# A rotary embedding kernel: six slabs in flight, and casts, products and sum inside the slab's own bytes

## The chip, the cores and the metric

The kernel runs on one core of a Trainium2 chip. The time is the device time of one execution in microseconds (us). Three runs of the kernel before took 162.06, 162.46 and 162.85 us; the median is 162.46.

The engines are called as in the profile: PE (TensorE), DVE (VectorE), ACT (ScalarE), POOL (GpSimd) and SP (SyncE). A letter q behind an engine's name stands for its sequencer, which waits and issues DMAs.

## What is computed

The input x has 16 batches of 512 positions with 16 heads of 64 values. In each head the two halves are rotated by the position's angles:

```python
x = x.reshape(batch, seq, num_heads, head_dim)
x1, x2 = x[..., :half_dim], x[..., half_dim:]
cos = cos[None, :, None, :]
sin = sin[None, :, None, :]
rotated = np.concatenate([x1 * cos - x2 * sin,
                          x1 * sin + x2 * cos], axis=-1)
```

Input and output are float32, 33.55 MB each. cos and sin have 512 x 32 values each.

## The kernel before

The work is cut into eight slabs of two batches. A slab is a tile of 128 partitions by 8192 float32 values (32 KB per partition, 4.194 MB in all); each partition holds eight consecutive positions of 1024 values, so that a slab is one contiguous stretch of DRAM. A slab is loaded by one DMA (line 64), worked on, and stored by one DMA from the same tile (line 141).

The pool of slabs has five places (`slots`). Loads 0 to 4 are issued at the start by SP, with the two small tables behind load 0. Load s + 5 is asked for after store s, into the same place, and so waits until store s has landed. Loads 0 to 5 are issued by SP and loads 6 and 7 by POOL (line 62). Stores are issued by ACT, in ACT's own instruction stream.

Lines 81 to 103 make the table `tab`: cos and sin, for all 128 partitions, as bf16, the sine with a minus sign in the half where it is needed. That is done once, by POOL, PE and DVE.

A slab is worked on in passes (lines 118 to 121): slabs 0, 6 and 7 in two passes of four positions (4096 values per partition), called 0a, 0b, 6a, 6b, 7a and 7b in this document, and slabs 1 to 5 in one of eight (8192 values). A pass has five instructions:

- a cast by ACT from the float32 slab to a bf16 buffer `xb` (line 112, "cast 5" is that of slab 5);
- two products by DVE (line 133): `xb` times the sine goes to the first half of the pass's bytes in the slab (`t2`, seen as bf16), and `xb` times the cosine goes to `xb` itself;
- a sum by DVE (line 136) of `xb` and `t2` with its halves swapped, into `xb`;
- a widening by ACT from `xb` to the float32 slab (line 139, "copy 5").

There are two buffers `xb` of a whole slab (16 KB per partition each), so that the cast of slab s waits for the widening of slab s - 2.

The text asks for the cast of the next pass before the products of this one; each engine runs its instructions in a fixed list. The framework that builds the program makes these lists and the waits; on ACT it has put cast 1 ahead of both copies of slab 0, where the text has it between them, and it keeps to the text from there on.

The five and the two buffers take 5 x 32 + 2 x 16 = 192 KB per partition.

Of the kernel before, what the change touches and what calls it, by code (L numbers as in the profile page):

```python
# [2 lines left out]

# [4 lines left out]


@with_exitstack  # L10
def kernel(
    ctx: ExitStack,
    tc: tile.TileContext,
    x: bass.AP,
    cos: bass.AP,
    sin: bass.AP,
    num_heads: int,
    out: bass.AP,
):
    nc = tc.nc  # L20
    P = nc.NUM_PARTITIONS

    batch, seq, dim = x.shape
    nh = num_heads
    hd = dim // nh
    half = hd // 2
    bf16 = mybir.dt.bfloat16
    f32 = mybir.dt.float32

    nb = 2  # L30
    slots = 5
    nslabs = batch // nb
    rpp = nb * seq // P
    W = rpp * dim
    SP = seq // rpp
    TW = rpp * half

    out_flat = out.rearrange("b s h d -> b s (h d)")

    singles = ctx.enter_context(tc.tile_pool(name="singles", bufs=1))  # L40
    slabs = ctx.enter_context(tc.tile_pool(name="slabs", bufs=slots))
    xpool = ctx.enter_context(tc.tile_pool(name="xpool", bufs=2))
    psum = ctx.enter_context(tc.tile_pool(
        name="psum", bufs=1, space=bass.MemoryType.PSUM))


    def dram(t, s, a=0, n=W):
        return bass.AP(tensor=t.tensor, offset=t.offset + s * nb * seq * dim + a,
                       ap=[[W, P], [1, n]])


    def view(t, offset, *dims):
        return dataclasses.replace(t, offset=t.offset + offset,
                                   ap=[t.ap[0], *[list(d) for d in dims]])


    slab = {}


    def load(s):  # L60

        queue = nc.sync if s < nslabs - 2 else nc.gpsimd
        slab[s] = slabs.tile([P, W], f32, tag="slab", name="slab")
        queue.dma_start(out=slab[s], in_=dram(x, s))  # L64


    load(0)


    cos_sb = singles.tile([SP, TW], f32, tag="cos_sb")  # L70
    sin_sb = singles.tile([SP, TW], f32, tag="sin_sb")
    for t, src in ((cos_sb, cos), (sin_sb, sin)):
        nc.sync.dma_start(out=t, in_=bass.AP(  # L73
            tensor=src.tensor, offset=src.offset, ap=[[TW, SP], [1, TW]]))

    for s in range(1, slots):
        load(s)

    pick = singles.tile([SP, 2 * P], bf16, tag="pick")
    nc.gpsimd.memset(pick, 0.0)  # L82
    for g in range(2):
        part = view(pick, g * P, (SP, P // SP), (1, SP))
        nc.gpsimd.affine_select(  # L85
            out=part, in_=part, compare_op=mybir.AluOpType.not_equal,
            fill=1.0 - 2.0 * g, base=0, pattern=[[0, P // SP], [-1, SP]],
            channel_multiplier=1)

    tab1 = singles.tile([SP, 2 * TW], bf16, tag="tab1")  # L90
    for i, t in enumerate((cos_sb, sin_sb)):
        nc.gpsimd.tensor_copy(out=view(tab1, i * TW, (1, TW)), in_=t)  # L92

    acc = psum.tile([P, 2 * rpp * hd], f32, tag="acc")
    for i in range(2):
        for h in range(2):
            nc.tensor.matmul(  # L97
                view(acc, i * rpp * hd + h * half, (hd, rpp), (1, half)),
                view(pick, i * h * P, (1, P)),
                view(tab1, i * TW, (half, rpp), (1, half)),  # L100
                start=True, stop=True)
    tab = singles.tile([P, 2 * rpp * hd], bf16, tag="tab")
    nc.vector.tensor_copy(out=tab, in_=acc)  # L103

    xb = {}


    def cast(u):
        s, r, n = u
        if r == 0:  # L110
            xb[s] = xpool.tile([P, W], bf16, tag="xb", name="xb")
        nc.scalar.copy(out=view(xb[s], r * dim, (1, n * dim)),  # L112
                       in_=view(slab[s], r * dim, (1, n * dim)))

    passes = []
    for s in range(nslabs):
        n = rpp if 1 <= s < nslabs - 2 else rpp // 2  # L120
        passes += [(s, r, n) for r in range(0, rpp, n)]


    cast(passes[0])
    for i, (s, r, n) in enumerate(passes):
        if i + 1 < len(passes):
            cast(passes[i + 1])
        xs = view(slab[s], r * dim, (1, n * dim))
        xu = view(xb[s], r * dim, (1, n * dim))

        t2 = view(slab[s].bitcast(bf16), 2 * r * dim, (1, n * dim))
        for t, a in ((t2, rpp * hd), (xu, 0)):
            nc.vector.tensor_mul(  # L133
                out=t, in0=xu,
                in1=view(tab, a + r * hd, (hd, n), (0, nh), (1, hd)))
        nc.vector.tensor_add(  # L136
            out=xu, in0=xu, in1=view(t2, half, (hd, n * nh), (-half, 2), (1, half)))

        nc.scalar.copy(out=xs, in_=xu)  # L139
        if r + n == rpp:  # L140
            nc.scalar.dma_start(out=dram(out_flat, s), in_=slab[s])  # L141
            if s + slots < nslabs:
                load(s + slots)


# [1 line left out]
_INS = ['x', 'cos', 'sin', 'num_heads']  # L147
_OUTS = [((16, 512, 16, 64), 'float32')]

_NUMBERS = {'num_heads': 16}  # L150


# [26 lines left out]
```

## Time and profile before

| what | value |
|---|---|
| median of three runs | 162.46 us |
| span of the profiled execution | 160.2 us |
| around the span (median less span) | 2.3 us |
| ACT busy | 113.5 us, 71% of the span, 23 instructions |
| DVE busy | 108.6 us, 68%, 34 instructions |
| POOL busy, PE busy | 3.0 us, 1.0 us |
| moved by DMA | 67.24 MB, mean 420 GB/s |
| DMA time of SP's, ACT's and POOL's queues, share of 16 engines | 37.5%, 48.5%, 12.1% |
| cast or widening on ACT, 128 x 8192 | 7.02 us |
| one product or sum on DVE, 128 x 8192 | 4.43 us |

The profile is of one execution; its own time beside the span isn't recorded, so the median stands for it. Times in it count from the first instruction. "Busy" is the time in which an engine runs an instruction. The line "DMA" of the page gives the mean busy share of the 16 DMA engines in each of 40 slices, in tenths, where 9 is 90% or more. In the timeline a line has the start, the duration, the engine, the line of the kernel, the operation, the tiles and shapes, and in brackets the idle time before it with what ended it. A line for several instructions shows the time from the first start to the last end. "To landing" is the time from a DMA's issue to its last byte's arrival.

### The profile page before, as it was taken

The numbers are of one execution on the slowest core, as the hardware profiler recorded it, in microseconds if no ns is written. First come the engines' busy times: TensorE is split into PE (matmuls) and PEld (weight loads), VectorE is DVE, ScalarE is ACT, GpSimd is POOL, SyncE is SP. The second block draws the span as 40 slices with busy tenths as digits, with TensorE's granted clock in tenths as the row PEclk, the third lists the DMA queues.
The fourth block names the chain that finished last, engine by engine and source line by source line (L and its number), as shares of the span: only waits on it lengthen the run. The fifth ranks groups of instructions, "written<-read, shape, count | busy, mean of one in ns | idle before, by whom it ended". The sixth has DMA issues, their size and how long they took to land.

```text
span 160.2 us, 159 instructions
## 1 busy us (share of the span) xinstructions
PE 1.0 (1%) x4; PEld 0.5 (0%) x4; DVE 108.6 (68%) x34; ACT 113.5 (71%) x23; POOL 3.0 (2%) x11
## 2 busy tenths in 40 slices
PE   0002000000000000000000000000000000000000
PEld 0000000000000000000000000000000000000000
DVE  0001899999979979997997299919839499940000
ACT  3006929998999999899919995089995999553000
POOL 2001000000000000000010001000000000000000
DMA  7999999999999999999999999999999999999995
GB/s 246 409 393 426 393 450 466 393 417 491 401 393 426 491 393 409 499 401 393 483 434 393 450 466 393 426 483 401 409 491 409 393 475 442 393 442 475 393 426 229
DMA packets 2464, 67.24 MB, mean 420 GB/s; under 512 B 288, under 2 KB 416, under 8 KB 416
## 3 DMA queue, kind: packets, MB, share of 16 engines
q10 hardware_dynamic: 1152, 33.55, 48.5%
q1 hardware_dynamic: 1024, 25.30, 37.5%
q0 software_dynamic: 288, 8.39, 12.1%
HBM read 33.69 MB, written 33.55 MB: 420 GB/s over the span
## 4 chain that ended last, share of the span: by engine, by line
DMA 49%; ACT 28%; issue 8%; DVE 4%; SPq 1%; ACTq 0%; POOLq 0%
DMA slab<-in_x_dram 29%; DMA out_dram<-slab 20%; ACT slab L139 16%; ACT xb L112 12%; DVE xb L136 1%; DVE xb L133 1%; DVE slab L133 1%; SPq L73 1%; ACTq L141 0%; SPq L64 0%; POOLq L174 0%; ACTq L139 0%; POOLq L64 0%
## 5 line engine op out<-in xcount | busy, mean ns | idle before, releaser
L112 ACT CAST xb<-slab 128x4096 bf16<-128x4096 f32 (+1 forms) x11 | 56.6, 5155 | 27.8 <-DMA slab<-in_x_dram 26.5
L139 ACT CAST slab<-xb 128x4096 f32<-128x4096 bf16 (+1 forms) x11 | 56.6, 5154 | 3.5 <-DVE xb L136 3.5
L133 DVE TENSOR_TENSOR slab<-xb,tab 128x4096 bf16<-128x4096 bf16 (+1 forms) x11 | 35.9, 3260 | 17.3 <-ACT xb L112 17.2
L133 DVE TENSOR_TENSOR xb<-xb,tab 128x4096 bf16<-128x4096 bf16 (+1 forms) x11 | 35.9, 3261 | 0.3
L136 DVE TENSOR_TENSOR xb<-xb,slab 128x4096 bf16<-128x4096 bf16 (+1 forms) x11 | 35.9, 3261 | 0.3
L103 DVE CAST tab<-acc 128x1024 bf16<-128x1024 f32 x1 | 1.2, 1225 | 15.2 <-PE acc L97 15.2
L64 POOL DMA_DIRECT2D slab<-in_x_dram x2 | 1.2, 608 | 84.1 <-DMA out_dram<-slab 84.1
L112 ACT ACT_TABLE_LOAD x1 | 1.3, 1283 | 0.7 <-PEq L160 0.7
L97 PE MATMUL acc<-tab,pick 64*128 64x256 bf16 x4 | 1.0, 402 | 14.2 <-POOL tab L92 14.2
L92 POOL CAST tab<-cos_sb 64x256 bf16<-64x256 f32 x1 | 0.4, 389 | 12.1 <-DMA cos_sb<-in_cos_dram 12.1
L85 POOL TENSOR_SCALAR_AFFINE_SELECT pick<-pick 64x128 bf16<-64x128 bf16 x2 | 0.5, 285 | 0.1
L97 PEld LDWEIGHTS <-pick 64*128 64x128 bf16 x4 | 0.5, 122 | 14.2 <-issue 12.6
L92 POOL CAST tab<-sin_sb 64x256 bf16<-64x256 f32 x1 | 0.4, 394 | 0.0
L82 POOL MEMSET pick<- 64x256 bf16 x1 | 0.3, 304 | 0.3 <-POOLq L160 0.3
L160 POOL MEMSET const-float32-0.0<- 128x1 f32 x1 | 0.1, 103 | 0.2 <-issue 0.2
L160 POOL MEMSET const-bfloat16-1.0<- 128x1 bf16 x1 | 0.1, 107 | 0.0
L160 POOL MEMSET const-uint8-127<- 128x1 uint8 x1 | 0.1, 106 | 0.0
L160 POOL MEMSET const-float32-1.0<- 128x1 f32 x1 | 0.1, 103 | 0.0
## 6 DMA issues: line engine op xcount, KB each, us to landing
out_dram<-slab ACTq DMA_DIRECT2D x8, 4096.0 KB, 25.9
slab<-in_x_dram SPq DMA_DIRECT2D x6, 4096.0 KB, 26.6
slab<-in_x_dram POOLq DMA_DIRECT2D x2, 4096.0 KB, 24.9
cos_sb<-in_cos_dram SPq DMA_DIRECT2D x1, 64.0 KB, 12.5
sin_sb<-in_sin_dram SPq DMA_DIRECT2D x1, 64.0 KB, 12.3
```

Of the source, the lines that this page charges most:

```text
L64: queue.dma_start(out=slab[s], in_=dram(x, s))
L73: nc.sync.dma_start(out=t, in_=bass.AP(tensor=src.tensor, offset=src.offset, ap=[[TW, SP], [1, TW]]))
L82: nc.gpsimd.memset(pick, 0.0)
L85: nc.gpsimd.affine_select(out=part, in_=part, compare_op=mybir.AluOpType.not_equal, fill=1.0 - 2.0 * g, base=0, pattern=[[0, P // SP], [-1 ...
L92: nc.gpsimd.tensor_copy(out=view(tab1, i * TW, (1, TW)), in_=t)
L97: nc.tensor.matmul(view(acc, i * rpp * hd + h * half, (hd, rpp), (1, half)), view(pick, i * h * P, (1, P)), view(tab1, i * TW, (half, rpp) ...
L103: nc.vector.tensor_copy(out=tab, in_=acc)
L112: nc.scalar.copy(out=view(xb[s], r * dim, (1, n * dim)), in_=view(slab[s], r * dim, (1, n * dim)))
L133: nc.vector.tensor_mul(out=t, in0=xu, in1=view(tab, a + r * hd, (hd, n), (0, nh), (1, hd)))
L136: nc.vector.tensor_add(out=xu, in0=xu, in1=view(t2, half, (hd, n * nh), (-half, 2), (1, half)))
L139: nc.scalar.copy(out=xs, in_=xu)
L160: nc = _bacc.Bacc("TRN2", target_bir_lowering=False, num_devices=1)
```

## The change

The pool of slabs gets a sixth place, and loads 0 to 5 are issued at the start. Load 6 follows store 0 and load 7 follows store 1. The condition that picks the queue now reads `s < slots`, which is s < 6 as before.

The two bf16 buffers are removed. The float32 bytes of a pass in the slab are now seen as two halves of bf16 values, `lo` and `up`, each as long as the pass. The cast reads the float32 values and writes them as bf16 to `lo`, the first half of the same bytes. The first product, with the cosine, goes from `lo` to `up`; the second, with the sine, goes from `lo` to `lo`. The sum adds `up` and `lo` with its halves swapped, into `up`. The widening reads `up` and writes the float32 values over the whole of the pass's bytes. Buffers take 6 x 32 = 192 KB per partition.

```diff
-    slots = 5
+    slots = 6
...
-    xpool = ctx.enter_context(tc.tile_pool(name="xpool", bufs=2))
...
-        queue = nc.sync if s < nslabs - 2 else nc.gpsimd
+        queue = nc.sync if s < slots else nc.gpsimd
...
-    xb = {}
-    def cast(u):
-        s, r, n = u
-        if r == 0:
-            xb[s] = xpool.tile([P, W], bf16, tag="xb", name="xb")
-        nc.scalar.copy(out=view(xb[s], r * dim, (1, n * dim)),
-                       in_=view(slab[s], r * dim, (1, n * dim)))
...
+    def halves(u):
+        s, r, n = u
+        t = slab[s].bitcast(bf16)
+        return [view(t, (2 * r + i * n) * dim, (1, n * dim)) for i in range(2)]
+    def cast(u):
+        s, r, n = u
+        nc.scalar.copy(out=halves(u)[0], in_=view(slab[s], r * dim, (1, n * dim)))
...
-        xs = view(slab[s], r * dim, (1, n * dim))
-        xu = view(xb[s], r * dim, (1, n * dim))
-
-        t2 = view(slab[s].bitcast(bf16), 2 * r * dim, (1, n * dim))
-        for t, a in ((t2, rpp * hd), (xu, 0)):
+        lo, up = halves(u)
+        for t, a in ((up, 0), (lo, rpp * hd)):
             nc.vector.tensor_mul(
-                out=t, in0=xu,
+                out=t, in0=lo,
                 in1=view(tab, a + r * hd, (hd, n), (0, nh), (1, hd)))
         nc.vector.tensor_add(
-            out=xu, in0=xu, in1=view(t2, half, (hd, n * nh), (-half, 2), (1, half)))
+            out=up, in0=up, in1=view(lo, half, (hd, n * nh), (-half, 2), (1, half)))
-        nc.scalar.copy(out=xs, in_=xu)
+        nc.scalar.copy(out=view(slab[s], r * dim, (1, n * dim)), in_=up)
```

More of the change, by code (lines that the diff above doesn't have):

```diff
@@ L121 @@
         passes += [(s, r, n) for r in range(0, rpp, n)]
+    def halves(u):
[5 more added lines that the diff above has]
+        nc.scalar.copy(out=halves(u)[0], in_=view(slab[s], r * dim, (1, n * dim)))
     cast(passes[0])
-    for i, (s, r, n) in enumerate(passes):
+    for i, u in enumerate(passes):
+        s, r, n = u
         if i + 1 < len(passes):
             cast(passes[i + 1])
-        xs = view(slab[s], r * dim, (1, n * dim))
-        xu = view(xb[s], r * dim, (1, n * dim))
-        t2 = view(slab[s].bitcast(bf16), 2 * r * dim, (1, n * dim))
-        for t, a in ((t2, rpp * hd), (xu, 0)):
+        lo, up = halves(u)
+        for t, a in ((up, 0), (lo, rpp * hd)):
             nc.vector.tensor_mul(
-                out=t, in0=xu,
+                out=t, in0=lo,
                 in1=view(tab, a + r * hd, (hd, n), (0, nh), (1, hd)))
         nc.vector.tensor_add(
-            out=xu, in0=xu, in1=view(t2, half, (hd, n * nh), (-half, 2), (1, half)))
-        nc.scalar.copy(out=xs, in_=xu)
+            out=up, in0=up, in1=view(lo, half, (hd, n * nh), (-half, 2), (1, half)))
+        nc.scalar.copy(out=view(slab[s], r * dim, (1, n * dim)), in_=up)
         if r + n == rpp:
```

## The prediction

> **What bounds the kernel now.** I read the page's DMA lines first, then the rate in one long stretch, then the timeline for the places where ScalarE (ACT) waits. The page, slices of 4 us:
>
> ```profile
> DVE  0001899999979979997997299919839499940000
> ACT  3006929998999999899919995089995999553000
> ...
> DMA  7999999999999999999999999999999999999995
> GB/s 246 409 393 426 393 450 466 393 417 491 401 393 426 491 393 409 499 401 393 483 434 393 450 466 393 426 483 401 409 491 409 393 475 442 393 442 475 393 426 229
> ...
> HBM read 33.69 MB, written 33.55 MB: 420 GB/s over the span
> ```
>
> The DMA line is full from the second slice to the last but one, while VectorE (DVE) and ACT have holes. The stretches view gives the rate in the middle, in its last column:
>
> ```profile
> 20.00:152.00 132.00, 0.00 (x0) 0.00 (x0) 104.41 (x32) 105.65 (x21) 1.22 (x2) 1.00 1.00 433
> ```
>
> So one slab of 4.194 MB takes 4.194/0.433 = 9.7 us when it has the DMA engines to itself. Sixteen slab transfers (8 in, 8 out) are 155 us; the other 5 us of the 160.2 us span are the start and the last landing. The same bytes move after the change. Hence the floor: **nothing that only moves transfers about can win more than the fraction of a microsecond that the DMA line lacks in the middle; what can happen is that the DMA engines run dry.** Where are they closest to that? At the end, when the last store is issued. I need the two landing summaries (first the loads' line, then the stores' line) and the timeline from there back:
>
> ```profile
> DMA to landing us min/median/max: 12.6/24.9/60.8
> ```
>
> ```profile
> DMA to landing us min/median/max: 13.7/25.9/37.3
> ```
>
> ```profile
> 61.21 0.33 SPq L64 DMA_DIRECT2D slab<-in_x_dram  x1
> ...
> 66.34 0.34 ACTq L141 DMA_DIRECT2D out_dram<-slab  x1
> ```
>
> ```profile
> 23.54 7.02 ACT L112 CAST xb<-slab 128x8192 bf16<-128x8192 f32 x1 [3.04 <-DMA slab<-in_x_dram]
> ...
> 30.46 7.11 ACT L139 CAST slab<-xb 128x4096 f32<-128x4096 bf16 x2
> ...
> 79.90 0.69 POOL L64 DMA_DIRECT2D slab<-in_x_dram  x1 [65.41 <-DMA out_dram<-slab]
> 80.69 0.34 ACTq L141 DMA_DIRECT2D out_dram<-slab  x1
> ...
> 84.21 7.02 ACT L112 CAST xb<-slab 128x8192 bf16<-128x8192 f32 x1 [3.54 <-DMA slab<-in_x_dram]
> ...
> 104.83 3.60 ACT L112 CAST xb<-slab 128x4096 bf16<-128x4096 f32 x1 [6.69 <-DMA slab<-in_x_dram]
> ...
> 124.22 3.60 ACT L112 CAST xb<-slab 128x4096 bf16<-128x4096 f32 x1 [1.85 <-DMA slab<-in_x_dram]
> ...
> 141.91 3.60 ACT L139 CAST slab<-xb 128x4096 f32<-128x4096 bf16 x1 [3.46 <-DVE xb L136]
> 145.54 0.34 ACTq L141 DMA_DIRECT2D out_dram<-slab  x1
> ```
>
> What is to be seen: the first load, alone, lands 12.6 us after its issue (the loads' minimum), that is 9.7 plus 2.9 of lag. Store 7 is issued at 145.5 and lands 13.7 later (the stores' minimum), at 159.3; the span ends 0.9 after that. With an idle engine it would have needed only 12.6: it waited 1.1 us behind store 6. So **the cover is 1.1 us: store 7 may be issued until 146.6 at no cost; each microsecond later is one microsecond of time.** ACT and DVE reach 145.5 after waiting for loads 5, 6 and 7 (3.5, 6.7 and 1.9 us).
>
> **The change, part by part.**
>
> Sixth slab: load 5 no longer waits for store 0. Now it is issued at 61.2, when store 0 has landed. After, SP issues it at about 4.5, behind loads 0 to 4 in the same queue. That wins nearly nothing by itself: load 4, issued at about 4, is the one with the 60.8 us landing, at 64.8, so SP's queue is busy until then in any case. But loads 6 and 7 move: POOL issues load 6 when store 0 (not 1) has landed, at 61.7 instead of 79.9, and load 7 after store 1. The condition on the queue reads differently (s < 6 in both cases), so both stay with POOL. No DMA is added.
>
> From about 66 three queues have bytes to move at once: SP load 5, POOL load 6, ACT the stores. Before, there were two: store 0 took from 37.6 to 61.1 beside the loads, 23.5 = twice 9.7 plus 4.1; load 6 took 24.9 = twice 9.7 plus 5.5. Two queues share by halves. Three at once is not in the trace. Bounds for load 5: at best it lands as now, at 84.2 (POOL takes nothing from it); at worst it stands still while load 6 passes at half speed, 19.4 more, 103.6. I extend the halves to thirds, 29.1 us for a slab: load 5 moves from 63.5 to 66 at half speed (0.13 of it), the other 0.87 takes 25.3, to 91.3, and 1.2 to land: **92.5 instead of 84.2.** Load 6 ends just behind it, about 95 (now 104.8), load 7 about 114.5 (now 124.2).
>
> The Trainium skill ("DMA: Bandwidth & Descriptors", "Queues, rings and completion order") states that each DMA engine goes round the queue rows that have work, a packet at a time; by that the share is a third and load 5 lands at 92.5, and without it the sum would be that of now. In the trace SP and ACT together move 432 GB/s (44 to 61 us), POOL and ACT 429 (86 to 98). The same page ("Issuing engines are not separate DMA queues") holds that one more issuing engine brings no bandwidth, which speaks against this change: by it load 6 can only come earlier by making load 5 later; if a third queue had a rate of its own, both would land by 86 and the sum would be no change.
>
> No bf16 buffers: casts, products, sum and widening keep their count and shape.
>
> ```profile
> L112 ACT CAST xb<-slab 128x8192 bf16<-128x8192 f32 x5 | 35.1, 7018 | 7.9 <-DMA slab<-in_x_dram 6.6 <-ACT slab L139 1.3
> L139 ACT CAST slab<-xb 128x8192 f32<-128x8192 bf16 x5 | 35.1, 7015 | 0.0
> ...
> L133 DVE TENSOR_TENSOR xb<-xb,tab 128x8192 bf16<-128x8192 bf16 x5 | 22.1, 4425 | 0.2
> L133 DVE TENSOR_TENSOR slab<-xb,tab 128x8192 bf16<-128x8192 bf16 x5 | 22.1, 4425 | 7.3 <-ACT xb L112 7.3
> ```
>
> On DVE the in-place product and the one into another buffer both take 4425 ns, so 3 x 4.43 = 13.3 us a slab stays. ACT over its own input is not in the trace. It is the same instruction on the same elements, and both directions take 7.02, so I exclude a gain; the dearest conversion by element in the trace is DVE's evacuation, 1225 ns for 1024, which would make 9.8 us of 7.0 and ACT the bound at about 158 us. I take 7.02, the nearest row. The wait of a cast for the old buffer was 0.4 us, three times: nothing.
>
> What is queued behind the late cast: ACT runs in a fixed list, cast of the next pass, then widening of this one. Behind cast 5 stand copy 4, store 4 and all that follows. Sum, from 92.5: cast 5 to 99.5; copy 4 to 106.5, store issue 0.4, cast 6a to 110.5; DVE works on slab 5 from 99.5 to 112.8, so copy 5 waits 2.3 us and runs to 119.9, issue 0.4; cast 6b to 123.9, copy 6a to 127.5, cast 7a to 131.1, copy 6b to 134.7, issue 0.4, cast 7b to 138.7, copy 7a to 142.3; DVE works on 7b from 138.7 to 145.7; copy 7b to 149.3. **Store 7 goes at 149.3, 3.8 later than now; 1.1 of that is covered.** Lag with nothing else in the engines 2.9: 149.3 + 12.6 + 0.9 = 162.8 us of span, 2.6 more than now. By store 0's 4.1 it would be 164.0; I take 2.9, since by then the engines are empty. What lies around the span is taken from the median, 162.46 - 160.2 = 2.3 (the three runs lie from 162.06 to 162.85; the profiled one has no separate time on record): 162.8 + 2.3 = **165.1 us**.
>
> **Rivals.**
>
> No change by ACT's list, 162.5: the list puts cast 6b ahead of copy 5, as load 6 now lands long before it. That fills ACT's 2.3 us wait and starts DVE on 6b about 4 us earlier (it would wait from 119.8 to 123.9), so store 7 goes near 146; it decides from 146.6 down. Against: the list of now has cast 6b after copy 5.
>
> No change by the queues, 162.5: POOL's transfer gets less than its third, and load 5 lands 2.6 us earlier than I say, by 89.9. For it: load 6 had 5.5 of lag where store 0 had 4.1, so POOL's transfers start late. Against: once started it went at half speed like the others.
>
> Slower still, 168.5: the bf16 buffers also held the casts back (two slabs at most). Without them the list may run casts further ahead: the timeline shows cast 1 at 23.5 ahead of both copies of slab 0 at 30.5, against the text's order, so the list does not keep to the text. If cast 5 stands ahead of copy 3, then copy 3 and store 3 (7.4 us) wait for load 5 too: 92.5 + 56.7 of ACT work + 3.5 wait for DVE = 152.7, span 166.2. With slab 6's casts in front too, DMA runs dry already before store 3, and it is near 170.
>
> Faster, 161.5: between the first issue at 0.7 and the end, 160.2 - 0.7 - 155.2 - 2.9 - 0.9 = 0.5 us is all that the DMA engines lost. To win these and another 0.5 the rate would have to rise by 0.3%, and nothing shows that it can.
>
> **How the numbers follow.** Forecast 0.48; slower still 0.22; no change by the list 0.15, by the queues 0.10; faster 0.05. The difference that a measurement of this kernel can tell is about 0.5%, 0.8 us; so slower 0.70, same 0.25, faster 0.05. The range takes in no change at its low end, 162.2, and reaches 170.0 above. Outside are the faster case, the worst of the reordered lists, load 5 at 103.6 and dear in-place casts on ACT.
>
> **What would show it.** Load 5's cast (first whole cast after 80) starts near 92, with an ACT wait of 11 us before it instead of 3.5: right; at 84: the thirds are wrong. POOL's first DMA at 61.7, second at 87. ACT's order after 60 unchanged: right; a cast of slab 5 or 6 ahead of a copy of slab 3 or 4: the harder rival. Casts at 7.02: in place is free. A DMA slice below 9 just before the last ten microseconds, with store 7 issued near 149: the step to the end. If the DMA line is full to the end, there is no change.

## The result, and the profile after

The changed kernel took 163.8 us (median of six runs, from 163.4) against 162.54 for the kernel before in the same series; the ratio is 1.0081, with a 95% interval of 1.0056 to 1.0106. One run of each six came out 2% longer or more, as do some runs of most kernels here, and the ratios leave such runs out. The change makes the kernel slower by about 0.8%, 1.3 us; the forecast was 1.6% slower, 165.1 us. The profiled execution took 163.56 us, and its span is 161.8 us, so 1.8 us lie around the span.

The page of the changed kernel, the same lines as those of before:

```profile
DVE  0002899999899989989991000999991999991000
ACT  3007929999999999999500079995799999928000
...
DMA  7999999999999999999899999999999999996996
...
HBM read 33.69 MB, written 33.55 MB: 416 GB/s over the span
```

Two things are to be seen. ACT has one wide hole, 79 to 94 us, and DVE one behind it, 85 to 101 us, where before they had several small ones. And the DMA line has a 6 near its end, in the slice from 145.6 to 149.7 us by the start of the packets: the DMA engines ran dry for a moment. The stretches view shows the place (last two columns: share of the DMA engines, GB/s), first in the kernel before, then in the changed one:

```profile
148.00:152.00 4.00, 0.00 (x0) 0.00 (x0) 0.00 (x0) 0.00 (x0) 0.00 (x0) 1.00 0.93 401
```

```profile
144.00:148.00 4.00, 0.00 (x0) 0.00 (x0) 2.08 (x1) 1.84 (x1) 0.00 (x0) 1.00 1.06 459
148.00:152.00 4.00, 0.00 (x0) 0.00 (x0) 0.00 (x0) 1.77 (x1) 0.00 (x0) 1.00 0.66 279
152.00:156.00 4.00, 0.00 (x0) 0.00 (x0) 0.00 (x0) 0.00 (x0) 0.00 (x0) 1.00 0.93 401
```

From 148 to 152 they are busy for 0.66 of the time, where the kernel before has 0.93. This view counts a packet by its start, and a packet takes over 1 us, so it is coarse. The packets themselves say it exactly: the last one of store 6 ends at 149.26 and the first one of store 7 starts at 150.64, so that nothing moves for 1.4 us. In the kernel before, store 6 also ends at 149.26, but store 7 starts at 148.70, ahead of that. The span grew by 1.6 us (161.8 - 160.2). The timeline shows why:

```profile
61.77 0.69 POOL L63 DMA_DIRECT2D slab<-in_x_dram  x1 [47.47 <-DMA out_dram<-slab]
...
88.40 0.53 POOL L63 DMA_DIRECT2D slab<-in_x_dram  x1 [25.93 <-DMA out_dram<-slab]
93.97 7.02 ACT L121 CAST slab<-slab 128x8192 bf16<-128x8192 f32 x1 [15.00 <-DMA slab<-in_x_dram]
93.97 0.34 ACTq L139 DMA_DIRECT2D out_dram<-slab  x1
...
114.40 7.02 ACT L137 CAST slab<-slab 128x8192 f32<-128x8192 bf16 x1 [2.98 <-DVE slab L134]
...
146.16 3.60 ACT L137 CAST slab<-slab 128x4096 f32<-128x4096 bf16 x1 [3.56 <-DVE slab L134]
149.80 0.34 ACTq L139 DMA_DIRECT2D out_dram<-slab  x1
```

Loads 6 and 7 start 18 and 11 us earlier than before. Cast 5 starts at 94.0 instead of 84.2, after a wait of 15 us. From there on ACT or DVE is always at work, and where one waits it waits for the other; store 7 is issued at 149.8 instead of 145.5. The stores' summary now has a minimum of 11.1 us, which is store 7's:

```profile
DMA to landing us min/median/max: 11.1/23.0/43.3
```

149.8 + 11.1 + 0.9 = 161.8, the span.

Why load 5 is late is shown by the DMA queues from 68 to 84 us (q0 is POOL's, q1 SP's, q10 ACT's; the last column is the share of the 16 engines):

```profile
q0 software_dynamic: 72, 2.36, 34.7%
q1 hardware_dynamic: 70, 2.29, 33.3%
q10 hardware_dynamic: 70, 2.29, 33.2%
```

Three queues with work share by thirds. In the same stretch of the kernel before there are two:

```profile
q10 hardware_dynamic: 128, 3.67, 53.1%
q1 hardware_dynamic: 116, 3.28, 47.4%
```

### The profile page after: what moved, and what is told of

Same layout as the page of the kernel before. It is cut to its first block, busy times and chain, and to the rows that moved or that the text cites. A ratio compares the mean times of both kernels' runs of the same rounds, so it can differ in the third digit from the quotient of the medians.

```text
span 161.8 us, 157 instructions
## 1 busy us (share of the span) xinstructions
PE 1.0 (1%) x4; PEld 0.5 (0%) x4; DVE 108.5 (67%) x34; ACT 113.2 (70%) x23; POOL 3.0 (2%) x11
## 4 chain that ended last, share of the span: by engine, by line
ACT 34%; issue 23%; DMA 13%; DVE 12%; another core or an unknown queue 9%; SPq 1%; ACTq 0%
ACT slab L137 23%; DMA slab<-in_x_dram 13%; ACT slab L121 11%; DVE slab L131 8%; DVE slab L134 4%; SPq L72 1%; SPq L63 0%; ACTq L137 0%; ACTq L121 0%
## 5 line engine op out<-in xcount | busy, mean ns | idle before, releaser
L131 DVE TENSOR_TENSOR slab<-slab,tab 128x4096 bf16<-128x4096 bf16 (+1 forms) x22 | 71.7, 3261 | 22.2 <-ACT slab L121 21.7
L121 ACT CAST slab<-slab 128x4096 bf16<-128x4096 f32 (+1 forms) x11 | 56.6, 5153 | 29.3 <-DMA slab<-in_x_dram 29.3
L137 ACT CAST slab<-slab 128x4096 f32<-128x4096 bf16 (+1 forms) x11 | 56.6, 5154 | 6.6 <-DVE slab L134 6.5
L134 DVE TENSOR_TENSOR slab<-slab 128x4096 bf16<-128x4096 bf16 (+1 forms) x11 | 35.9, 3261 | 0.3
```

The lines of the kernel that those rows point to most:

```text
L121: nc.scalar.copy(out=halves(u)[0], in_=view(slab[s], r * dim, (1, n * dim)))
L131: nc.vector.tensor_mul(out=t, in0=lo, in1=view(tab, a + r * hd, (hd, n), (0, nh), (1, hd)))
L134: nc.vector.tensor_add(out=up, in0=up, in1=view(lo, half, (hd, n * nh), (-half, 2), (1, half)))
L137: nc.scalar.copy(out=view(slab[s], r * dim, (1, n * dim)), in_=up)
```

## The experiments

The theory of the forecast (theory 1): a third queue makes load 5 late, the work behind it becomes late as a whole, and the part of the delay of store 7 that store 6 does not cover is the loss. The first rival (theory 2): the work inside the slab's own bytes costs, by its instructions or by a new order on ACT. All ratios are to the kernel before, on the same chip.

**Two queues instead of three.**

```diff
-        queue = nc.sync if s < slots else nc.gpsimd
+        queue = nc.sync
```

> The changed kernel with loads 6 and 7 issued by SP, behind load 5 in the same queue; six slabs and the in-place work stay. Theory 1 (three queues share by thirds, load 5 comes 10 us late, and what ACT does after it comes late with it): with two queues load 5 lands near 84, cast 5 starts there, store 7 goes at 145 to 146, span 160.2 to 160.7, ratio to the kernel before 0.997 to 1.003. Theory 2 (work inside the slab's own bytes costs, by the instructions or by the list in which a store stands behind the next cast): it stays at the changed kernel's 1.008.

Measured: 162.04 us, ratio 0.9976 (0.9959 to 0.9992), span 160.1. The timeline:

```profile
84.12 7.02 ACT L121 CAST slab<-slab 128x8192 bf16<-128x8192 f32 x1 [5.16 <-DMA slab<-in_x_dram]
...
103.50 3.60 ACT L121 CAST slab<-slab 128x4096 bf16<-128x4096 f32 x1 [5.45 <-DMA slab<-in_x_dram]
...
144.24 0.34 ACTq L139 DMA_DIRECT2D out_dram<-slab  x1
```

Load 5 is back at 84.1, though six slabs are in flight, all work is in place and the order on ACT is that of the changed kernel. Store 7 goes at 144.2. This is theory 1's result, and theory 2 falls. The version is also 0.2% faster than the kernel before, barely clear of the scatter.

**In place alone.** Five slabs, with the queues and waits of before.

```diff
-    slots = 6
+    slots = 5
...
-        queue = nc.sync if s < slots else nc.gpsimd
+        queue = nc.sync if s < nslabs - 2 else nc.gpsimd
```

> The changed kernel with five slabs, so that loads 5, 6 and 7 wait for stores 0, 1 and 2 as before; only the in-place part of the change is left. Theory 1: load 5 at 84, load 6 at 105, load 7 at 124, store 7 near 145.5, ratio to the kernel before 0.997 to 1.003. Theory 2: 1.008.

Measured: 162.18 us, ratio 0.9984 (0.996 to 1.0008); cast 5 at 84.1, casts 6a and 7a at 104.8 and 124.2, store 7 at 145.5. Working in the slab's own bytes costs nothing that can be measured. The groups of the changed kernel by shape say the same of the instructions: the cast and the widening of 128 x 8192 over their own input take 7016 ns each, against 7018 and 7015.

**Load 5 stays late, but the tail is shortened.** In the text, the cast of 6b moves ahead of the work of pass 5.

```diff
-        if i + 1 < len(passes):
+        if i + 1 < len(passes) and (s, r) != (nslabs - 2, 0):
             cast(passes[i + 1])
+        if s == nslabs - 3:
+            cast(passes[i + 2])
```

> The changed kernel with cast 6b ahead of copy 5 in ACT's list; queues as changed. Theory 1 says that only the time of store 7 counts: load 5's cast stays at 94, but DVE has 6b 3.6 us earlier, store 7 goes at 146.5, and that is early enough: span 160.2 to 160.6, ratio 0.997 to 1.003. A rival (three queues at once, or store 3 issued late behind cast 5, cost the DMA engines time by themselves): it stays at 1.006 to 1.008.

> The kernel with cast 6b ahead of copy 5 once more, for its profile. Load 5's cast near 94 after a wait of 15 us on ACT, as in the changed kernel; store 7 at 146.5 (the changed kernel: 149.8); the DMA line full to the end; span 160.2 to 160.6.

> The kernel with cast 6b ahead of copy 5 once more: cast 5 near 94 after an ACT wait of some 15 us, store 7 at 146.5, DMA line full to the end, span 160.1 to 160.6.

Measured: 162.15 us, ratio 0.9989 (0.9972 to 1.0007), and in the last series 162.25, 0.9988 (0.9962 to 1.0015). The first two profiled executions had spans of 165.0 and 163.8 us and are not read here; the third has a span of 160.5, and its DMA line is full to the end:

```profile
DMA  7999999999999999999999999999999999999993
```

```profile
94.18 7.02 ACT L121 CAST slab<-slab 128x8192 bf16<-128x8192 f32 x1 [15.12 <-DMA slab<-in_x_dram]
94.19 0.34 ACTq L141 DMA_DIRECT2D out_dram<-slab  x1
...
146.78 0.34 ACTq L141 DMA_DIRECT2D out_dram<-slab  x1
```

Three queues, load 5 at 94 and an ACT wait of 15 us are all still there, and so is store 3, issued only with cast 5. Store 7 goes 3.0 us earlier, and the loss is gone. So none of these costs time by itself that can be seen; the time of store 7 does.

**The same delay without the change.** The kernel before, with the last widening done twice, wholly or for 2048 of its 4096 values.

```diff
+        if i + 1 == len(passes):
+            nc.scalar.copy(out=xs, in_=xu)
         if r + n == rpp:
```

> The kernel before, with the last widening (7b, 3.6 us on ACT) done twice, so that store 7 goes at 149.1 instead of 145.5 and nothing else moves. By the forecast's cover of 1.1 us: span 162.7, ratio 1.015. By the changed kernel's 11.1 us from issue to landing (cover 2.6): span 161.1, ratio 1.004 to 1.006. If the late store is not the cause of the longer time at all: 1.000.

> The kernel before with 2048 values of the last widening done twice (1.9 us on ACT), store 7 at 147.4. By a cover of 2.6 us (11.1 us from issue to landing): no change, ratio 0.998 to 1.002. By the forecast's cover of 1.1: span 0.8 us longer, ratio 1.005.

Measured: with the whole widening, store 7 at 149.0, span 161.0, ratio 1.0037 (1.0015 to 1.0059). With the half, store 7 at 147.9, ratio 0.9998 (0.9968 to 1.0028). The stretch view of the first shows a hole at the same place as in the changed kernel, and its stores' summary the same minimum:

```profile
148.00:152.00 4.00, 0.00 (x0) 0.00 (x0) 0.00 (x0) 0.95 (x1) 0.00 (x0) 1.00 0.66 279
```

```profile
DMA to landing us min/median/max: 11.1/26.2/37.6
```

By its packets the hole is shorter here, 0.5 us against 1.4, and store 7 goes 0.8 us earlier than in the changed kernel. A late store 7 alone, in a kernel that is otherwise that of before, costs what theory 1 says. The cover is 13.7 - 11.1 = 2.6 us and not the 1.1 of the forecast: by the ratios a store 2.4 us later costs nothing that can be seen, and one 3.5 us later costs 0.4%, with 0.8 us of span in the profile.

The profile with the half has a span of 161.0 too, just what a cover of 1.1 would give. But its view has no hole:

```profile
148.00:152.00 4.00, 0.00 (x0) 0.00 (x0) 0.00 (x0) 0.00 (x0) 0.00 (x0) 1.00 1.01 434
```

In that execution the transfers were late before store 7 was issued at all: store 5's last packet ends at 140.4, against 139.6 in the kernel before. So the span is not the store's doing, and the ratio, whose interval ends at 1.0028, speaks against the 1.005 that a cover of 1.1 asks for.

**Filling ACT's wait.** The 15 us hole looks as if it were the loss. Here copy 4, which is ready at 85.8, goes ahead of cast 5. Store 4 was meant to go with it, but the cast stands ahead of it in the edit, and in the trace it is issued at 94.3, with cast 5; only store 3 moves forward, to 85.8.

```diff
-        if i + 1 < len(passes):
+        if i + 1 < len(passes) and s != nslabs - 4:
             cast(passes[i + 1])
...
         nc.scalar.copy(out=view(slab[s], r * dim, (1, n * dim)), in_=up)
+        if s == nslabs - 4:
+            cast(passes[i + 1])
```

> The changed kernel with copy 4 ahead of cast 5 in ACT's list, so that 7 us of ready work and store 4 go into ACT's 15 us wait for load 5. If what counts is ACT's wait as such, store 7 goes up to 7 us earlier and the loss is gone: ratio 1.000. If the tail hangs on load 5 through DVE (cast 5 at 94, products and sum of slab 5 to 114.4, copy 5, then cast 6b), ACT only gets a new wait before copy 5 and store 7 stays at 149.8: ratio 1.006 to 1.009.

Measured: 164.06 us, ratio 1.0092 (1.0064 to 1.0119): no gain over the changed kernel.

```profile
85.76 7.02 ACT L137 CAST slab<-slab 128x8192 f32<-128x8192 bf16 x1 [6.54 <-DVE slab L134]
...
94.33 7.02 ACT L121 CAST slab<-slab 128x8192 bf16<-128x8192 f32 x1 [1.56 <-DMA slab<-in_x_dram]
...
114.81 7.02 ACT L137 CAST slab<-slab 128x8192 f32<-128x8192 bf16 x1 [9.96 <-DVE slab L134]
121.74 3.60 ACT L121 CAST slab<-slab 128x4096 bf16<-128x4096 f32 x1
...
150.22 0.34 ACTq L141 DMA_DIRECT2D out_dram<-slab  x1
```

ACT's wait moved: most of it is now the 10 us before copy 5, which needs DVE's work on slab 5, which needs cast 5, which needs load 5. Cast 6b stands where it stood.

**Both cures together**, SP's loads and the early cast 6b.

> Loads 6 and 7 on SP and cast 6b ahead of copy 5, both together. Each alone keeps the DMA engines full, so both together can win nothing more: store 7 earlier than 144.2, the span still 160.1, ratio 0.996 to 1.000. If engine time were worth anything here, it would be faster than the kernel with SP's loads alone (0.9976).

Measured: ratio 0.9979 (0.9955 to 1.0004), the same as with SP's loads alone. The profiled execution had a span of 170.2 us, so store 7's time is not read from it, and that part of the expectation stays untested.

**No work at all.** Casts, products, sums and widenings are left out: each slab is stored as it was loaded, with six slabs and all loads on SP.

> Leaves out the whole rotation: each slab is stored as it was loaded (six slabs, all loads on SP, the tables still made). If the DMA engines alone set the time of the kernel before, this is no faster than its best runs by more than the 0.5 us that they lost: span 159.5 to 160.2, ratio 0.994 to 1.000. If engine work were still a part of the kernel before, it would be clearly faster: below 0.99.

Measured: 162.12 us, ratio 1.0007 (0.9979 to 1.0035), span 160.4. Without the rotation the kernel is not faster. The floor that the forecast worked out from 433 GB/s is confirmed for these sixteen transfers: the kernel before stands on it, within the scatter of the runs, and the most that any run here gained is the 0.2% of SP's loads.

## Why the prediction was right, and what was mis-sized

The mechanism was right, step by step.

- That load 5 gains nothing from its early issue, and loses by the third queue: thirds were taken, 34.7, 33.3 and 33.2% were measured, and load 5's last packet ends at 91.2 us, where the forecast had 91.3. From there to landing the forecast took 1.2 us without a row for it; measured are 2.8, so that it landed at 93.9 instead of 92.5. POOL's loads were forecast at 61.7 and 87, and issued at 61.8 and 88.4. A detail was wrong without effect: SP issues load 5 at 13.2 and not at 4.5, after a wait of 8.7 us that ends when load 0 has landed; the bytes of load 4 are in front until about 64 anyway.
- That in-place work costs nothing: the experiment with five slabs shows it within the scatter, and the durations agree.
- The sum on ACT: store 7 at 149.3 forecast, 149.8 measured; the wait of copy 5 for DVE 2.3 and 3.0 us. That store 7 came so close is in part luck: load 5 was 1.5 us later than forecast, and the way from cast 5 to store 7 1.0 us shorter, 55.8 us against 56.8. The sum had charged ACT 0.4 us for each of three store issues on that way; in the trace each comes just after the next cast has begun and holds nothing up. ACT's wait before cast 5 is 15.0 us, where the forecast had 11: besides the late landing, ACT comes to it 1.7 us earlier than before, and gains nothing by it.
- That the DMA engines run dry just before the last store: shown by the packets. That nothing else costs more than the scatter: shown by the early cast 6b and by the kernel without work.

The size was twice too large, by two terms of the last sum. **The lag of store 7 with nothing else in the engines** was taken as 2.9 us beside 9.7, from the first load of the program: 12.6 from issue to landing. Measured is 11.1, or 1.4 of lag, in the changed kernel and in the kernel before with the doubled widening. The first load is a poor model for the last store: its packets take 10.9 us from the first start to the last end, those of store 7 9.9. Why the first load is slower is not shown. The same error made the cover 1.1 us instead of 2.6. The other term is **what lies around the span**: 2.3 us were taken, from a median that did not belong to the profiled execution; it is 1.8 in every run on record. The sum with the measured terms, 149.8 + 11.1 + 0.9 + 1.8 = 163.6, is the profiled time.

A rule of the Trainium skill would have done better here than the row: "DMA: Bandwidth & Descriptors", "Anatomy of one DMA", gives a fit for one DMA issued from GpSimd, 2.0 us and the bytes at 436 GB/s. For a slab that makes an estimate of 11.6 us; store 7, issued from ACT, measured 11.1.

The rivals. "No change by ACT's list" did not happen, but its mechanism is real: with cast 6b ahead of copy 5, by hand, the loss is gone. "No change by the queues" fell: POOL's queue gets its full third. "Slower still" did not happen: no cast moved ahead of a widening that the forecast had in front of it. Its sum of 152.7 also lacks the store issues that the main sum charged. "Faster" did not happen either. The list did change in one thing that was not foreseen: every store's issue but the last now stands behind the next cast. In the kernel before only stores 5 and 6 do, which are issued at 115.39 and 131.37, just after casts 6b and 7b began; so that list did not keep to the text throughout. Store 3 now goes at 94.0, with cast 5, instead of 80.7. It cost nothing that can be seen, since ACT's queue was busy with stores 1 and 2 until 106.9. No run here shows what such a delay costs where the queue is empty.

## What to carry to other kernels

Where the DMA engines are full from start to end, look for the place where they can run dry, here ahead of the last store, and reckon for every change by how much it moves that issue and how much of it the transfer in front covers. One more buffer that lets one more queue start early was no gain here: queues with work shared the engines equally, so a transfer that nobody needs yet takes its share from the one that is waited for next. With all loads in one queue, in the order of need, load 5 was back on time. An engine's long wait is not the loss by itself: filling it with other work changed nothing, while moving one 3.6 us cast in the tail removed the loss.

## What the runs showed of the hardware

Three queues were served equally, also POOL's beside SP's and ACT's, at an unchanged total: 433 GB/s from 60 to 80 us in the changed kernel as in the one before. A 4.194 MB store issued just after the engines had run dry landed after 11.1 us, the first load of the program after 12.6 in the kernel before and 12.4 in the changed one. A cast from float32 to bf16 into the first half of its own bytes, and a widening from the second half over the whole, take as long as between two buffers (7016 ns against 7018 and 7015 for 128 x 8192).
